# The first stage of a gated-MLP trunk kernel rebuilt: load order, the first modulation tile, and a written order on three engines

## The chip, the cores and the metric

One core of one Trainium2 chip runs the kernel. The metric is the device time of one execution in microseconds, median of the runs.

## The reference, cut to what matters

The input x has 2048 rows (tokens) of 1024 columns, in float32. With depth 1 the trunk is one layer with the chunked gMLP mixer:

```
mod = silu(c) @ ada_w + ada_b                  # 3072 values: shift, scale, gate
h   = rmsnorm(x, norm_g) * (1 + scale) + shift
u, v, z = split(h @ w_in, 3)                   # w_in: 1024 x 6144
u = gelu(u);  v = layernorm(gelu(v))
v = spatial mixing of v in chunks of 128 tokens, 8 heads
x = x + gate * ((u * v * silu(z)) @ w_out)
out = rmsnorm(x, final_g)
```

The stage that is changed is the beginning: from x, c and ada_w to h for the first 512 tokens, and the first products of h with w_in.

## The kernel before, in words

Every float32 product on TensorE is made from three matmuls (`mm3`, L175): each operand is split into a rounded part hi and a rest lo (`split`: hi by ACT, lo by DVE), and hi\*hi, hi\*lo and lo\*hi are summed in PSUM. The large products follow Strassen's scheme on quadrants of h and of the weights (A11, A12, A22 and the sums S1 to S4); the tokens are taken in two halves of 1024, and each of these in two halves of 512 (`HT`). The width of 1024 is cut into `KD` = 8 columns k of 128, of which k < 4 (`KH`) belong to A11 and the others to A12.

The first stage is the pool named "start". Its parts:

- **Rows.** c, norm_g and ada_b are loaded as rows and transposed by TensorE to columns; ACT makes c_act = silu(c) of them.
- **Modulation.** For each column k the 1024 x 128 blocks of ada_w for shift and scale are loaded by two transfers (`mod_load`, 1 MB in all, in three tiles used in turn). `mod_sum` multiplies the eight 128-row blocks by c_act and sums them: two products, by ACT (by DVE for k = 0), six multiply-adds and one add on DVE. Two small matmuls with a column of ones sum over the partitions into a PSUM tile pm; `mod_cols` turns pm into one scale and one shift column with three DVE instructions.
- **x.** Four chunks of 128 tokens (`load_half`) are normalised (`normalize_steps`: squares on ACT, a power on GpSimd, a scaling on DVE) and transposed by TensorE, column by column (`transpose_half`). `take_a1` copies the transposed column from PSUM; `modulate` (L249) applies scale and shift on ACT, and `put` splits the result h(k) into sh and sl.
- **Products.** For every k the weights of one 512-wide block of v and of two 128-wide blocks of u are loaded (`first_load`) and split (`first_split`). Four chunks and two units of u take three matmuls each, 18 matmuls a step, into six PSUM banks. After k = 3 the banks are evicted by ACT and started again for A12.

The order on DVE and ACT in this stage is the order of the program text (`tc.manual_schedule`, L747); TensorE's order and the order of the loads on SP's queue are made by the planner of the tile framework. In that text the sum for column k+2 stands in step k, the columns of k+1 are made in step k, and five x columns are transposed ahead of step 0. Loads are issued on SP's one queue: the rows, two ada tiles, four x chunks, then weights and ada tiles in turn; the second half of x (x2) is loaded in step 4.

Behind the stage come the second product group (`v1`, tiles named p_v), the normalisation of x2, and the rest of the program, which the edit doesn't touch.

Of the kernel before, what the change touches and what calls it, by code (L numbers as in the profile page):

```python
# [17 lines left out]
P = 128  # L18
# [4 lines left out]
def kernel(  # L23
# [192 lines left out]
    def mod_sum(j, aw):  # L216


        am = s_slot(A22, j % KH, "hl"[j // KH], F32, f"am_{j}", (P, 2, 2, P))
        for k in range(KD):  # L220
            a, ck = am[:, k % 2], c_act[:, k:k + 1]
            if k < 2 and j:
                nc.scalar.activation(a, aw[:, :, k, :], AF.Copy, scale=ck)
            elif k < 2:
                nc.vector.tensor_scalar(a, aw[:, :, k, :], ck, None, op0=ALU.mult)
            else:
                nc.vector.scalar_tensor_tensor(a, aw[:, :, k, :], ck, a, op0=ALU.mult, op1=ALU.add)
            if k in (3, 5, 6):
                yield None
        nc.vector.tensor_tensor(am[:, 0], am[:, 0], am[:, 1], op=ALU.add)  # L230
        pm = aux_bank(f"pm_{j}")
        for s in (1, 0):
            nc.tensor.matmul(
                pm[:, s:s + 1], lhsT=am[:, 0, s, :], rhs=ones[:, 0:1], start=True, stop=True
            )
        yield pm

    def mod_cols(cols, j, pm):
        nc.vector.tensor_tensor(
            mscale[:, j:j + 1], pm[:, 1:2], cols[:, R_SC + j:R_SC + j + 1], op=ALU.add  # L240
        )
        nc.vector.tensor_scalar(
            mscale[:, j:j + 1], mscale[:, j:j + 1], 1.0, cols[:, R_G + j:R_G + j + 1],
            op0=ALU.add, op1=ALU.mult,
        )
        nc.vector.tensor_tensor(
            mshift[:, j:j + 1], pm[:, 0:1], cols[:, R_SH + j:R_SH + j + 1], op=ALU.add
        )
# [461 lines left out]
    with tc.tile_pool(name="start", bufs=1) as st:  # L710
        nc.sync.dma_start(rows[R_C:R_C + KD, :], c.rearrange("o (k p) -> (o k) p", p=P))
        nc.sync.dma_start(
            rows[R_G:R_G + KD, :], norm_g.rearrange("o (k p) -> (o k) p", p=P)
        )
        nc.sync.dma_start(
# [3 lines left out]
        ps_r = aux_bank("ps_rows")  # L719
        nc.tensor.transpose(ps_r[:, :NR], rows[:NR, :], ident[:NR, :NR])  # L720
        nc.scalar.activation(c_act, ps_r[:, R_C:R_C + KD], AF.Silu)
        nc.vector.tensor_copy(cols, ps_r[:, :NR])
# [11 lines left out]
        v0, v1 = groups[0]  # L734

        def take_a1(k):
            ps = transpose_half(xh, 0, k, acc_bank if k < 5 else aux_bank)
            t = s_slot(S4, k % KH, "hl"[k // KH], F32, f"a1_{k}")
            if k == 0:
                modulate(t, ps, k)  # L740
            elif k in (1, 3):
                nc.vector.tensor_copy(t, ps)
            else:
                nc.scalar.activation(t, ps, AF.Copy)
            a1.append(t)

        with tc.manual_schedule(engines={mybir.EngineType.DVE, mybir.EngineType.Activation}):  # L747
            *_, pm[0] = mod_sum(0, aws[0])
# [571 lines left out]
```

## Time and profile before

| | before |
|---|---|
| time, median of 3 runs | 1341.31 us (1339.07 to 1345.71) |
| the profiled execution's own time | 1339.62 us |
| its span, first to last instruction | 1337.5 us |
| PE busy | 1309.9 us (98%) |
| DVE busy | 1073.9 us (80%) |
| ACT busy | 681.7 us (51%) |

The span is what the rows below are timed in: 0 is the first instruction of the profiled execution. PE is TensorE's matmuls, PEld its weight loads, DVE is VectorE, ACT is ScalarE, POOL is GpSimd and SPq the queue from which loads and stores are issued. A matmul's duration contains its pipeline; how fast matmuls follow is read from the distance of their starts. An instruction's line is often that of a helper: all splits are L166 and L167, all products L176 to L178.

### The profile page before, as it was taken

The page shows a single profiled execution, that of the slowest core. Times are in us where ns is not written, and L with a number is a line of the kernel's source. Part 1 is how long each engine was busy: PE and PEld are TensorE (multiplying, and loading weights), DVE is VectorE, ACT ScalarE, POOL GpSimd, SP SyncE. Part 2 cuts the span into 40 slices and gives each one's busy share as a digit, 9 for nine tenths or more (in the row PEclk, how much of TensorE's full clock was granted, in tenths as well). Part 3 has the DMA queues.
Part 4 walks back from the last instruction along what each step waited for, and adds up shares of the span by engine and source line. Part 5 has one row for each costly group of instructions (what it writes and reads, how often), then busy time and mean ns, then how long its engine had stood idle before and what let it go on. Part 6 is the DMA issues. An engine that isn't in the chain of part 4 may idle for free.

```text
span 1337.5 us, 17181 instructions
## 1 busy us (share of the span) xinstructions
PE 1309.9 (98%) x6066; PEld 1087.3 (81%) x6066; DVE 1073.9 (80%) x1784; ACT 681.7 (51%) x1169; POOL 25.0 (2%) x42
## 2 busy tenths in 40 slices
PE   5999999999999999999999999999999999999997
PEld 4878878888888888888888888888888888888876
DVE  6889978888888888978678889887789944757974
ACT  5775445766555537534345545544543424344553
POOL 0000001000000000000000000000000000000101
PEclk9999999999999999999999999999999999999999
DMA  9871657456765547442244345433339722335723
GB/s 320 274 263 56 227 193 239 149 171 203 232 231 186 177 154 238 168 135 104 102 142 133 116 163 176 158 111 118 122 124 311 257 95 95 99 120 213 252 105 126
DMA packets 156798, 229.23 MB, mean 171 GB/s; under 512 B 9188, under 2 KB 91172, under 8 KB 153384
## 3 DMA queue, kind: packets, MB, share of 16 engines
q1 hardware_dynamic: 156712, 228.14, 50.0%
q8 instruction: 47, 0.77, 0.2%
q14 instruction: 39, 0.32, 0.1%
HBM read 160.47 MB, written 67.64 MB: 171 GB/s over the span
## 4 chain that ended last, share of the span: by engine, by line
PE 76%; DVE 4%; DMA 2%; ACT 1%; issue 1%; POOL 0%; POOLq 0%; ACTq 0%
PE p_z L178 7%; PE p_z L177 7%; PE p_z L176 7%; PE po L178 7%; PE po L177 7%; PE po L176 7%; PE p_u L178 6%; PE p_u L177 6%; PE p_u L176 6%; PE pmix_u L550 4%; PE p_v L176 3%; PE p_v L178 3%; PE p_v L177 3%; DMA vn<-v_dram 1%; DMA sl<-h_dram 1%
## 5 line engine op out<-in xcount | busy, mean ns | idle before, releaser
L176 PE MATMUL p_v<-hi_p_v,sh 128*128 128x512 f32 x416 | 162.8, 392 | 0.1
L177 PE MATMUL p_v<-lo_p_v,sh 128*128 128x512 f32 x416 | 162.5, 391 | 0.0
L178 PE MATMUL po<-hi_o,gl 128*128 128x512 f32 x416 | 161.9, 389 | 0.5 <-DVE gl L167 0.5
L178 PE MATMUL p_v<-hi_p_v,sl 128*128 128x512 f32 x416 | 162.2, 391 | 0.0
L176 PE MATMUL po<-hi_o,gh 128*128 128x512 f32 x416 | 161.9, 389 | 0.0
L177 PE MATMUL po<-lo_o,gh 128*128 128x512 f32 x416 | 161.8, 389 | 0.0
L166 ACT ACTIVATE gh<-gr 128x1024 fp32r<-128x1024 f32 x52 | 55.0, 1059 | 132.5 <-PE po L177 123.2
L166 ACT ACTIVATE hi_p_v<-b_v 128x512 fp32r<-128x512 f32 x104 | 65.0, 630 | 106.7 <-PE p_v L178 89.8
L167 DVE TENSOR_TENSOR gl<-gr,gh 128x1024 fp32r<-128x1024 f32 x52 | 63.6, 1223 | 60.4 <-ACT gh L166 60.2
L167 DVE TENSOR_TENSOR lo_p_v<-b_v,hi_p_v 128x512 fp32r<-128x512 f32 x104 | 70.0, 688 | 37.2 <-ACT hi_p_v L166 36.8
L176 PEld LDWEIGHTS p_v<-hi_p_v,sh 128*128 128x128 f32 x416 | 78.1, 188 | 17.4 <-DVE c_v L479 1.0
L178 PEld LDWEIGHTS po<-hi_o,gl 128*128 128x128 f32 x416 | 78.1, 188 | 17.0 <-DVE gl L167 1.0
L176 PEld LDWEIGHTS po<-hi_o,gh 128*128 128x128 f32 x416 | 78.1, 188 | 16.6 <-ACT gh L166 0.3
L177 PEld LDWEIGHTS p_v<-lo_p_v,sh 128*128 128x128 f32 x416 | 78.1, 188 | 16.5 <-issue 0.2
L177 PEld LDWEIGHTS po<-lo_o,gh 128*128 128x128 f32 x416 | 78.1, 188 | 16.2
L178 PEld LDWEIGHTS p_v<-hi_p_v,sl 128*128 128x128 f32 x416 | 78.1, 188 | 16.0
L536 ACT ACTIVATE vn<-vn,lm,lr 128x256 f32<-128x256 f32 x128 | 67.7, 590 | 27.4 <-DMA vn<-v_dram 18.1
L176 PE MATMUL p_u<-sh,hi_p_u 128*128 128x512 f32 x196 | 76.2, 389 | 0.0
L177 PE MATMUL p_u<-sl,hi_p_u 128*128 128x512 f32 x196 | 76.2, 389 | 0.0
L178 PE MATMUL p_u<-sh,lo_p_u 128*128 128x512 f32 x196 | 76.2, 389 | 0.0
L176 PE MATMUL p_z<-sh,hi_p_z 128*128 128x512 f32 x192 | 75.0, 391 | 0.0
L178 PE MATMUL p_z<-sh,lo_p_z 128*128 128x512 f32 x192 | 75.0, 391 | 0.0
(220 smaller groups left out, 3081.3 us busy)
## 6 DMA issues: line engine op xcount, KB each, us to landing
gr<-g_dram SPq DMA_DIRECT2D x26, 1024.0 KB, 4.8
b_v<-in_gm_w_in_dram SPq DMA_DIRECT2D x18, 1024.0 KB, 5.5
vn<-v_dram SPq DMA_DIRECT2D x16, 1024.0 KB, 6.1
raw_u<-in_gm_w_in_dram SPq DMA_DIRECT2D x16, 1024.0 KB, 5.0
raw_z<-in_gm_w_in_dram SPq DMA_DIRECT2D x16, 1024.0 KB, 5.1
v_dram<-c_v SPq DMA_DIRECT2D x44, 256.0 KB, 2.1
g_dram<-c_u SPq DMA_DIRECT2D x37, 256.0 KB, 2.1
aw<-in_ada_w_dram SPq DMA_DIRECT2D x16, 512.0 KB, 5.4
```

The costliest lines, as they stand in the source:

```text
L166: nc.scalar.activation(hi, src, AF.Copy)
L167: nc.vector.tensor_tensor(lo, src, hi.bitcast(F32), op=ALU.subtract)
L176: nc.tensor.matmul(ps, lhsT=sh, rhs=mh, start=first, stop=False)
L177: nc.tensor.matmul(ps, lhsT=sh, rhs=ml, start=False, stop=False)
L178: nc.tensor.matmul(ps, lhsT=sl, rhs=mh, start=False, stop=last)
L536: nc.scalar.activation(vt[:, ch, :], vt[:, ch, :], AF.Identity, bias=lm[:, ch:ch + 1], scale=lr[:, ch:ch + 1],)
L550: nc.tensor.matmul(pm[:, i * P:(i + 1) * P], lhsT=vt[:, m * (NCH // 2) + i, f * P:(f + 1) * P], rhs=spT[:, u.j, :], start=True, stop=True,)
```

## The change

The x chunks are loaded first, the rows go to ACT's queue, the first ada tile is loaded in four parts (scale before shift) and summed by TensorE alone: eight blocks times a c_act column, accumulated in PSUM. Column 1 is summed by both engines: DVE takes blocks 0 to 4, TensorE 5 to 7 and the two partial sums. The columns' additions of 1 are made once, and the shift column is added by ACT. For columns 0 and 1, hi of h is written by ACT directly from the transposed x in PSUM, and DVE makes the float32 h beside it (`h_at_once`); for the others ACT makes h from PSUM and h is then split (`h_in_turn`). The sum for column k+1 is finished in step k, and TensorE transposes column k+1 in step k too. The order on DVE, ACT and TensorE is that of the text. x2 is loaded in step 6 instead of step 4.

```diff
     def mod_load(pool, j):
...
-        for s in range(2):
-            nc.sync.dma_start(aw[:, s], ada_v[:, :, s * D + j * P:s * D + (j + 1) * P])
+        parts = [slice(0, KH), slice(KH, KD)] if j == 0 else [slice(0, KD)]
+        for s in (1, 0):
+            for ks in parts:
+                nc.sync.dma_start(aw[:, s, ks], ada_v[:, ks, s * D + j * P:s * D + (j + 1) * P])
...
+    def mod_init(j, by_act):
+        am[j] = s_slot(A22, j % KH, "hl"[j // KH], F32, f"am_{j}", (P, 2, 2, P))
+        for k in range(2):
+            src, ck = aws[j][:, :, k, :], c_act[:, k:k + 1]
+            if by_act:
+                nc.scalar.activation(am[j][:, k], src, AF.Copy, scale=ck)
             else:
+                nc.vector.tensor_scalar(am[j][:, k], src, ck, None, op0=ALU.mult)
+
+    def mod_acc(j, ks):
+        for k in ks:
+            a = am[j][:, k % 2]
+            nc.vector.scalar_tensor_tensor(
+                a, aws[j][:, :, k, :], c_act[:, k:k + 1], a, op0=ALU.mult, op1=ALU.add
+            )
+
+    def mod_add(j):
+        nc.vector.tensor_tensor(am[j][:, 0], am[j][:, 0], am[j][:, 1], op=ALU.add)
+
+    def mod_total(j, direct, parts):
+        pm[j] = aux_bank(f"pm_{j}")
         for s in (1, 0):
+            terms = [(aws[j][:, s, k, :], c_act[:, k:k + 1]) for k in direct]
+            terms += [(am[j][:, i, s, :], ones[:, 0:1]) for i in range(parts)]
+            for n, (w, m) in enumerate(terms):
+                nc.tensor.matmul(
+                    pm[j][:, s:s + 1], lhsT=w, rhs=m, start=n == 0, stop=n == len(terms) - 1
+                )
+
+    def mod_cols(j):
+        nc.vector.tensor_scalar(
+            mscale[:, j:j + 1], pm[j][:, 1:2], cols[:, R_SC + j:R_SC + j + 1],
+            cols[:, R_G + j:R_G + j + 1], op0=ALU.add, op1=ALU.mult,
         )
+        nc.scalar.activation(
+            mshift[:, j:j + 1], pm[j][:, 0:1], AF.Identity, bias=cols[:, R_SH + j:R_SH + j + 1]
         )
...
     with tc.tile_pool(name="start", bufs=1) as st:
-        nc.sync.dma_start(rows[R_C:R_C + KD, :], c.rearrange("o (k p) -> (o k) p", p=P))
+        nc.scalar.dma_start(rows[R_C:R_C + KD, :], c.rearrange("o (k p) -> (o k) p", p=P))
...
+        xh = load_half(st, 0)
         aws, wf, pm = {}, {}, {}
-        for k in range(2):
+        for k in range(3):
             aws[k] = mod_load(st, k)
-        xh = load_half(st, 0)
-        for k in range(3):
-            if k == 2:
-                aws[k] = mod_load(st, k)
             wf[k] = first_load(k)
...
+        def h_at_once(k):
+            hi, lo, a = h_slots(k)
+            nc.vector.tensor_scalar(
+                a, psx[k], mscale[:, k:k + 1], mshift[:, k:k + 1], op0=ALU.mult, op1=ALU.add
+            )
+            yield
+            modulate(hi, psx[k], k)
+            nc.vector.tensor_tensor(lo, a, hi.bitcast(F32), op=ALU.subtract)
+
+        def h_in_turn(k):
+            hi, lo, a = h_slots(k)
+            modulate(a, psx[k], k)
+            split(hi, lo, a)
...
+        manual = {mybir.EngineType.DVE, mybir.EngineType.Activation, mybir.EngineType.PE}
+        with tc.manual_schedule(engines=manual):
...
             for ch, xt in enumerate(xh):
+                normalize_x(xt, f"0_{ch}")
+                if ch < 3:
+                    turn_x(0, [ch])
+            mod_total(0, range(KD), 0)
+            turn_x(0, [3])
+            mod_cols(0)
+            take_psx(1)
+            steps = h_at_once(0)
+            next(steps)
+            w_v = split_w(wf[0][0], "wfv_0", (P, FB))
+            for _ in steps:
+                pass
+            ws.append((w_v, split_w(wf[0][1], "wfu_0", (P, NF, P))))
             for k in range(KD):
...
                 if k == 4:
-                    x2 = load_half(st, 1)
                     v1.load(0, 0, "raw0")
-                    v1.load(1, 0, "raw1")
...
+                if k == 0:
+                    for n in range(3):
+                        for ch in range(4):
+                            chunk(k, ch, [n])
+                        if n == 1:
+                            turn_x(1, range(4))
+                    mod_init(1, False)
+                    mod_acc(1, range(2, 5))
+                    mod_total(1, range(5, KD), 2)
+                    ws.append(first_split(1, wf[1]))
+                    mod_cols(1)
+                    for j in range(NF):
+                        unit(k, j)
+                    for _ in h_at_once(1):
+                        pass
+                    mod_init(2, True)
+                    mod_acc(2, range(2, 4))
+                    continue
+                if k + 1 < KD:
+                    take_psx(k + 1)
+                    turn_x(k + 1, range(4))
+                    mod_acc(k + 1, range(4, KD))
+                    mod_add(k + 1)
+                    ws.append(first_split(k + 1, wf[k + 1]))
+                if k == KD - 2:
+                    x2 = load_half(st, 1)
+                    v1.load(1, 0, "raw1")
+                if 2 <= k < KD - 2:
+                    mod_init(k + 2, True)
+                for ch in range(3):
+                    chunk(k, ch)
+                if k == 1:
+                    chunk(k, 3)
+                if k + 1 < KD:
+                    mod_total(k + 1, (), 1)
+                    mod_cols(k + 1)
+                    if 2 <= k < KD - 2:
+                        mod_acc(k + 2, range(2, 4))
+                    h_in_turn(k + 1)
+                    if k == 1:
+                        mod_init(k + 2, True)
+                        mod_acc(k + 2, range(2, 4))
+                if k > 1:
+                    chunk(k, 3)
                 for j in range(NF):
+                    unit(k, j)
```

`turn_x` transposes chunks of one column, `chunk` and `unit` are the three matmuls of one chunk or one unit, `h_slots` takes the tiles of h(k).

## Rows read from the trace of the kernel before

**Rows 1.** The page's busy time: engine, us (share of the span), instructions.

```profile
PE 1309.9 (98%) x6066; PEld 1087.3 (81%) x6066; DVE 1073.9 (80%) x1784; ACT 681.7 (51%) x1169; POOL 25.0 (2%) x42
```

**Rows 2.** Busy time by stretches: stretch, length, engines, granted clock, DMA share, GB/s.

```profile
7.00:7.50 0.50, 0.00 (x0) 0.00 (x0) 0.21 (x1) 0.00 (x0) 0.00 (x0) 1.00 1.14 345
...
13.50:14.00 0.50, 0.00 (x0) 0.00 (x0) 0.30 (x1) 0.50 (x3) 0.46 (x1) 1.00 1.01 418
...
22.00:26.00 4.00, 3.56 (x9) 2.85 (x10) 3.62 (x11) 2.90 (x7) 0.00 (x0) 1.00 1.12 349
...
26.00:61.00 35.00, 35.00 (x173) 29.31 (x172) 31.09 (x82) 26.54 (x50) 0.00 (x0) 1.00 0.91 299
```

**Rows 3.** Timeline of all engines, 0 to 17 us: start, duration, engine, line, operation.

```profile
0.74 0.40 SPq L711 DMA_DIRECT2D rows<-in_c_dram  x1
...
1.89 3.75 SPq L213 DMA_DIRECT2D aw<-in_ada_w_dram  x4
...
7.29 0.61 DVE L225 TENSOR_SCALAR am<-aw,c_act 128x256 f32<-128x256 f32 x2 [3.33 <-DMA aw<-in_ada_w_dram]
...
10.79 0.93 PEld L233 LDWEIGHTS pm<-ones,am 128*128 128x128 f32 x4 [7.41 <-DVE am L230]
...
12.12 1.06 ACT L155 ACTIVATE sq<-x 128x1024 bf16<-128x1024 f32 x1 [8.39 <-DMA x<-in_x_dram]
...
15.30 1.33 PE L267 MATMUL psx<-ident,x 128*128 128x128 f32 x5 [3.50 <-DVE r_m L147]
...
16.96 1.32 PE L267 MATMUL psx<-ident,x 128*128 128x128 f32 x5 [0.33 <-DVE r_m L147]
```

**Rows 4.** Timeline of PE, 22 to 62 us: first product to the next stage.

```profile
22.44 0.80 PE L176 MATMUL p<-hi_wfv,sh 128*128 128x512 f32 x1 [0.68 <-ACT sh L166]
...
25.96 0.40 PE L178 MATMUL p<-hi_wfv,sl 128*128 128x512 f32 x1
...
28.24 0.50 PE L233 MATMUL pm<-ones,am 128*128 128x1 f32 x4
28.60 0.64 PE L267 MATMUL psx<-ident,x 128*128 128x128 f32 x4
28.99 0.48 PE L176 MATMUL p<-hi_wfv,sh 128*128 128x512 f32 x1
...
61.04 0.39 PE L176 MATMUL p_v<-hi_p_v,sh 128*128 128x512 f32 x1
```

**Rows 5.** Timeline of ACT, 20 to 46 us.

```profile
20.95 0.78 ACT L251 ACTIVATE a<-psx,mshift,mscale 128x512 f32<-128x512 f32 x1 [2.11 <-PE psx L267]
...
29.77 0.62 ACT L166 ACTIVATE hi_wfv<-wfv 128x512 fp32r<-128x512 f32 x1
...
30.59 0.90 ACT L223 ACTIVATE am<-aw,c_act 128x256 f32<-128x256 f32 x2
31.39 0.81 ACT L251 ACTIVATE a<-a,mshift,mscale 128x512 f32<-128x512 f32 x1
32.23 0.63 ACT L166 ACTIVATE sh<-a 128x512 fp32r<-128x512 f32 x1
...
42.83 2.04 ACT L483 ACTIVATE c_v<-p 128x512 f32<-128x512 f32 x4
...
45.70 0.66 ACT L166 ACTIVATE hi_wfv<-wfv 128x512 fp32r<-128x512 f32 x1
```

**Rows 6.** Timeline of DVE, 28 to 33 us.

```profile
28.23 0.68 DVE L167 TENSOR_TENSOR sl<-a,sh 128x512 fp32r<-128x512 f32 x1
28.83 0.15 DVE L239 TENSOR_TENSOR mscale<-pm,cols 128x1 f32<-128x1 f32 x1
...
29.21 1.67 DVE L227 SCALAR_TENSOR_TENSOR am<-aw,c_act,am 128x256 f32<-128x256 f32 x4
...
32.19 0.87 DVE L227 SCALAR_TENSOR_TENSOR am<-aw,c_act,am 128x256 f32<-128x256 f32 x2
```

**Rows 7.** Timeline of ACT: the squares of the second half of x.

```profile
63.92 1.04 ACT L155 ACTIVATE sq<-x 128x1024 bf16<-128x1024 f32 x1
```

More of the change, by code (lines that the diff above doesn't have):

```diff
@@ L734 @@
         v0, v1 = groups[0]
[L736 to L748, printed above, removed]
-            mod_cols(cols, 0, pm[0])
-            sums = mod_sum(1, aws[1])
-            for ch, xt in enumerate(xh):
-                norm = normalize_steps(xt, f"0_{ch}")
-                next(norm)
-                pm[1] = next(sums)
-                next(norm)
-            ws = [first_split(k, wf[k]) for k in range(2)]
-            for k in range(5):
-                take_a1(k)
-                if k == 0:
-                    put(0, A11, 0, a1[0])
+        ws, psx = [], {}
@@ new lines, in take_psx, with turn_x, h_slots @@
+        def take_psx(k):
+            psx[k] = (acc_bank if k == 0 else aux_bank)(f"psx_0_{k}")
+            return psx[k]
+        def turn_x(k, chs):
+            for ch in chs:
+                nc.tensor.transpose(
+                    psx[k][:, ch * P:(ch + 1) * P], xh[ch][:, k * P:(k + 1) * P], ident
+                )
+        def h_slots(k):
+            i = A11 if k < KH else A12
+            hi = s_slot(i, k % KH, "h", F32R, f"sh_0_{i}_{k % KH}")
+            lo = s_slot(i, k % KH, "l", F32R, f"sl_0_{i}_{k % KH}")
+            S[i][k % KH] = (hi, lo)
+            a1.append(s_slot(S4, k % KH, "hl"[k // KH], F32, f"a1_{k}"))
+            return hi, lo, a1[k]
@@ new lines, in h_at_once, with chunk @@
+        def h_at_once(k):
+            hi, lo, a = h_slots(k)
+            nc.vector.tensor_scalar(
+                a, psx[k], mscale[:, k:k + 1], mshift[:, k:k + 1], op0=ALU.mult, op1=ALU.add
+            )
+            yield
[5 more added lines that the diff above has]
+            split(hi, lo, a)
+        def chunk(k, ch, passes=range(3)):
+            sh, sl = S[A11 if k < KH else A12][k % KH]
+            cs = slice(ch * P, (ch + 1) * P)
+            hi, lo = ws[k][0]
+            for n in passes:
+                l, r = ((sh, hi), (sh, lo), (sl, hi))[n]
+                nc.tensor.matmul(
+                    first[ch], lhsT=l[:, cs], rhs=r, start=k % KH == 0 and n == 0,
+                    stop=k % KH == KH - 1 and n == 2,
+                )
@@ new lines, in unit @@
+        def unit(k, j):
+            sh, sl = S[A11 if k < KH else A12][k % KH]
+            hi, lo = ws[k][1]
+            mm3(first[4 + j], hi[:, j], lo[:, j], sh, sl, k % KH == 0, k % KH == KH - 1)
+        manual = {mybir.EngineType.DVE, mybir.EngineType.Activation, mybir.EngineType.PE}
+        with tc.manual_schedule(engines=manual):
+            ps_r = aux_bank("ps_rows")
+            nc.tensor.transpose(ps_r[:, :NR], rows[:NR, :], ident[:NR, :NR])
+            nc.scalar.activation(c_act, ps_r[:, R_C:R_C + KD], AF.Silu)
+            nc.vector.tensor_copy(cols, ps_r[:, :NR])
+            nc.vector.tensor_scalar(
+                cols[:, R_SC:R_SC + KD], cols[:, R_SC:R_SC + KD], 1.0, None, op0=ALU.add
+            )
+            take_psx(0)
+            for ch, xt in enumerate(xh):
+                normalize_x(xt, f"0_{ch}")
[11 more added lines that the diff above has]
+            ws.append((w_v, split_w(wf[0][1], "wfu_0", (P, NF, P))))
@@ L790 @@
                     first = [acc_bank(f"p{k // KH + 1}_{j}") for j in range(4 + NF)]
-                sh, sl = S[i][k % KH]
-                edges = k % KH == 0, k % KH == KH - 1
-                for ch in range(4):
-                    cs = slice(ch * P, (ch + 1) * P)
-                    mm3(first[ch], sh[:, cs], sl[:, cs], *ws[k][0], *edges)
+                if k == 0:
[16 more added lines that the diff above has]
+                    continue
```

54 lines of the change are left out of this document (3 added, 51 removed).

## The prediction

> **What bounds the kernel now.** I read the page first, then the busy time by stretches, then the order of the work on each engine up to 62 us. TensorE is busy 1309.9 of the 1337.5 us of the span [rows 1], so all that any change of order can give back is 27.6 us, and most of that lies at the head. The stretches show it: from 22 to 26 us PE is busy for 3.56 of 4.00, from 26 to 61 for 35.00 of 35.00 [rows 2]. The first matmul of the stage starts at 22.44 and the first one of the stage behind it at 61.04 [rows 4]; everything behind 61.04 is untouched by the edit, so the question is where 61.04 goes. It is the sum of two things: when the first matmul starts, and how closely the eight steps k = 0..7 follow.
>
> Both parts have their own limit. The start waits for data and for a serial chain: ada_w lands and DVE begins at 7.29, x only at 12.12, behind it in the one queue, PE transposes from 15.30 [rows 3]. The steps are limited by PE itself: 28.99 to 61.04 for k = 1..7 is 4.58 us a step [rows 4], where 18 matmuls at 0.228 (25.96 to 28.24, ten of them [rows 4]) make 4.10 and the rest is pm and transposes. DVE is close behind: 31.09 of 35 us [rows 2].
>
> **The start after the change.** The x loads take the first place in the queue, at 0.74 instead of behind the row loads and ada_w. Fixed cost of a load: the 1.05 MB of the first ada tile went out at 1.89, were used at 7.29, and take 3.04 us at 345 GB/s, which leaves 2.4 [rows 2, 3]. So the first x chunk (0.52 MB at 418 GB/s, 1.25 us) is there at 0.74 + 2.4 + 1.25 = 4.4. From the start of its squares to its first transpose it was 12.12 to 15.30, 3.2 us; the next chunk followed 1.65 behind [rows 3]. The written order puts chunks 0 to 2 ahead of mod_total(0): 4.4 + 3.2 + 2 x 1.65 + 0.3 for the transpose = 11.2. The first ada tile is there by 0.74 + 2.4 + 5.0 + 3.0 = 11.2, its scale half 1.5 earlier, so the load is no later than PE needs it. The three row loads move to ACT's queue; their issue (0.74 to 1.89, 1.2 us [rows 3]) and the table load end before x lands, so they cost nothing, and if x came early they would cost at most those 1.2.
>
> What DVE did in 3.4 us is now PE's: 8 blocks, 2 sums, two passes each (the trace shows 4 records for the two products of one pm) = 32 passes. At the high level of the clock a pass is 0.09 (28.24 to 28.60 for four), at the low level 0.23 by the four at 10.79 to 11.72 [rows 3, 4]. Which level holds? Matmuls start 0.44 apart from 22.44 to 25.96 (eight) and 0.228 apart behind that [rows 4]: those are the 1.2 and 2.4 GHz levels, although the granted-clock column reads 1.00 in both stretches [rows 2]. Bounds of the 32 passes: 2.9 and 7.4. I take 0.18, twice the high-level pass, hence 5.8, and no slow matmuls behind: pm_0 is done at P = 17.0. Behind P come the two column operations (0.3, an estimate from the 0.15 at 28.83 [rows 6] and a handover), hi of the weights (0.62, as at 29.77 [rows 5]) and hi of h straight from PSUM (0.78, as at 20.95 [rows 5]): first matmul at P + 1.7 = 18.7, 3.7 earlier than before. That is the gain.
>
> **The steps after the change.** Call S(k) the moment at which hi of h(k) is ready. Step 0: 12 matmuls 2.74, the transposes of chunk column 1 at 0.39 (28.60 to 28.99 [rows 4]), then pm_1 with 20 passes, 1.8: P + 6.6; DVE's part (lo of h and of w, two products, three sums: 4.5 from P) lies beside it. Then columns 0.3, hi 0.78: S(1) = P + 7.7.
>
> From there the written order makes a ring over DVE and ACT, because pm(k+1) is now summed, used and turned into h(k+1) within one step; before, pm ran a step ahead. Ring: lo of h(k) on DVE 0.60 (28.23 to 28.83), four sums, add, lo of both weights 2.98 (29.21 to 32.19) [rows 6], scale column and handover 0.2, modulate 0.84 and hi 0.63 on ACT (31.39, 32.23 [rows 5]), handover 0.05: 5.3 us. PE's work of the step is 18 x 0.228 + pm 0.36 + transposes 0.39 = 4.85, so PE now waits about 0.45 a step (at mod_total, with chunk 3, both units and the next transposes queued behind it, which nothing but h(k+1) waits for), and it pays seven times 0.39 for transposes behind the first matmul where it paid three.
> In steps 1 and 2 the order has no sums ahead: ACT's two products (0.80, 30.59 to 31.39 [rows 5]) and two more sums (0.83) come into the ring, less lo of h that lies beside the products: 0.05 + 0.80 + 0.83 + 2.98 + 0.2 + 1.47 = 6.3 each. In step 4 six banks are evicted on ACT ahead of the weight splits: 2.87 (42.83 to 45.70), then hi of both weights 0.82, products 0.80, shift column 0.2, modulate and hi 1.47 [rows 5]: 6.2. Before, the same eviction cost PE nothing, since pm was a step ahead.
> So S(7) = P + 7.7 + 2 x 6.3 + 3 x 5.3 + 6.2 = P + 42.4. Step 7: 0.65 until lo is ready, then 16 x 0.228 = 3.65. The stage ends at P + 46.7 = 63.7, against 61.04: 2.7 us later. The start gives 3.7, the steps lose 6.4.
>
> Taken from DVE: one of three column operations per step (0.15 to 0.21) and the two copies; the ring already leaves them out. The ada reloads wait for tiles that are read a little later, but each has 5 us or more until its use; cost nothing, at worst one transfer of 3.0 once. The second half of x moves from k = 4 to k = 6, behind the last transposes: issue at about S(6) = 54 (SP holds the stores behind it for so long; they free tiles that nothing asks for before the next stage), last chunk 54 + 2.4 + 5.0 = 61.4; in the old order its squares start 2.9 behind the stage's end (63.92 [rows 7]), so at 66.6: hidden by 5 us.
>
> The profiled execution took 1339.62 us, 1.7 under the median of 1341.31. 1339.6 + 2.7 = 1342.3 on its scale; on the median's scale **1344.0 us**.
>
> **The rivals.**
> *The ring doesn't bind (faster).* If DVE and ACT kept up, PE would set the pace: P + 1.7 + 6.3 + 6 x 4.85 + 4.1 = P + 41.2. With the clock up halfway through the 32 passes (16 x 0.18 + 16 x 0.09 = 4.3, P = 15.5) that is 56.7, 4.3 earlier: 1337.0. With all passes at 0.09 it is 55.3: 1335.6, the most that the change can give. For it: PE was never seen waiting from 26 to 61. Against it: then no ring was closed within a step, and its members are measured.
> *The clock rises early, the ring stays.* P = 15.5, stage end 62.2: 1342.5. For it: the passes follow one another without a gap. Against it: the PE busy share before 22.44 was high too (transposes), and the matmuls behind it were slow.
> The Trainium skill (TensorE: Matmul & The Clock Gate, Part 1: The HAM clock gate) has the gate opened by sustained PE activity, which speaks for this rival; its Part 4: PE-mode transpose says that transposes don't count as busy in the same way, and the trace agrees with that, since the matmuls at 22.44 came at 0.44. No run here shows how one-column passes count.
> *Slower: the clock stays low until the dense matmuls have run for a while.* Place: pm_0 and step 0. Passes at 0.23 put P at 18.6, and eight matmuls at 0.44 instead of 0.228 add 1.7: stage end 67.0, 6.0 later, 1347.3. It decides from the point where S(1) lies beyond 26.9. For it: the 0.93 for four passes at 10.79 and the slow eight at 22.44 [rows 3, 4].
> *The second half of x is late.* It must now cross the queue in 7 us; if the 1 MB weight loads that wait for ada tiles stand ahead of it in the queue (two, 3.0 each by the rate above), it lands at 67.4, about 1 behind its use, and PE, which meets the transposes in order, waits for the chain of 3.2: 1345 to 1348.
>
> **How the numbers follow.** Forecast 0.50, its own range 1341 to 1347.5; ring not binding 0.12; early clock 0.15; low clock 0.15; late x 0.08. About 0.5%, 6.7 us, is what a measurement of this kernel can tell from no change: under 1334.6 is faster, over 1348.0 slower. Faster needs the very limit of the first rival (0.03 of its 0.12, and 0.01 for what I have not seen); slower gets 0.04 of the forecast, 0.06 of the low clock and 0.03 of the late x. That is faster 0.04, slower 0.13, no change 0.83. The range goes from the first rival's 1337.0 to 1350.0, the low clock with 0.4 us more in each of the seven rings.
>
> **What would show it.** First matmul of the stage near 18.7; the first x squares near 4.4; 32 passes between 11 and 17; DVE or ACT named as PE's releaser once a step, with 5.3 between the starts of steps 3, 5 and 6 and over 6 in 1, 2 and 4; the stage behind starting near 63.7. A first matmul before 16, or steps of 4.85, would make the prediction wrong towards faster; PE waiting for x transposes behind 64, towards slower.

## The result and the profile after

The changed kernel takes 1353.72 us (median of 4 runs, 1353.43 to 1354.29), the kernel before 1341.40 (4 runs, 1339.07 to 1345.71): ratio 1.0098, 95% interval 1.0083 to 1.0113. It is 12.3 us slower, where 2.7 were forecast, and beyond the 1350.0 at which the range ended. The profiled execution took 1354.29 us with a span of 1352.5, 15.0 more than before.

Busy time, as in [rows 1]:

```profile
PE 1321.5 (98%) x6110; PEld 1094.8 (81%) x6110; DVE 1069.1 (79%) x1758; ACT 679.0 (50%) x1168; POOL 24.7 (2%) x42
```

PE is busy 11.6 us longer with only 44 instructions more. The sum doesn't tell why; the distances of the starts do. Timeline of PE (start, duration, line, tile; in brackets the wait ahead of it), answering to [rows 3, 4]:

```profile
6.06 0.28 PE L793 MATMUL ps_rows<-ident,rows 32*128 32x32 f32 x1 [6.06 <-DMA rows<-in_ada_b_dram]
9.26 0.47 PE L747 MATMUL psx<-ident,x 128*128 128x128 f32 x1 [2.92 <-DVE r_m L147]
...
12.56 6.83 PE L249 MATMUL pm<-c_act,aw 128*128 128x1 f32 x32
19.24 0.45 PE L747 MATMUL psx<-ident,x 128*128 128x128 f32 x1
21.71 2.08 PE L780 MATMUL p<-hi_wfv,sh 128*128 128x512 f32 x4 [2.01 <-ACT sh L263]
...
27.55 0.72 PE L249 MATMUL pm<-c_act,aw 128*128 128x1 f32 x6
...
32.36 0.78 PE L780 MATMUL p<-hi_wfv,sh 128*128 128x512 f32 x1
...
74.42 0.39 PE L176 MATMUL p_v<-hi_p_v,sh 128*128 128x512 f32 x1
```

The first product comes at 21.71, only 0.73 earlier than before; step 1 starts at 32.36, 3.37 later; the stage behind starts at 74.42 instead of 61.04. So 13.4 of the 15.0 us arise in this stage. Of the rest, 1.2 is a longer wait for DVE in the second half of x (2.1 us against 0.9); the remaining 0.4 is not traced.

The stretches (engine columns PE, PEld, DVE, ACT, POOL, then granted clock, DMA share, GB/s), as [rows 2]:

```profile
12.00:19.00 7.00, 6.71 (x32) 6.71 (x33) 1.05 (x3) 0.00 (x0) 0.55 (x1) 1.00 1.14 355
...
21.50:27.50 6.00, 5.79 (x16) 4.68 (x17) 3.67 (x9) 1.28 (x4) 0.00 (x0) 1.00 0.67 212
27.50:29.70 2.20, 2.20 (x22) 2.15 (x21) 0.00 (x0) 0.00 (x0) 0.00 (x0) 1.00 0.00 0
...
30.60:33.90 3.30, 3.30 (x12) 2.60 (x11) 2.45 (x5) 2.40 (x5) 0.00 (x0) 0.50 1.00 296
...
36.00:74.00 38.00, 34.11 (x158) 24.90 (x157) 28.75 (x66) 25.19 (x51) 0.00 (x0) 1.00 0.76 247
```

Three things are to be seen. While TensorE sums column 0 (12 to 19 us) DVE and ACT do next to nothing, and while it sums column 1 (27.5 to 29.7) everything else stands still. Behind the passes of column 1 the granted clock is 0.50, the 1.2 GHz level, and there the products start 0.43 apart (30.80 to 31.23 to 31.66). The twelve products behind column 0 start 0.43 apart too, though the column reads 1.00 for them (21.5 to 27.5): this trace has no record of the clock ahead of 27.18, the column shows 1.00 where there is none, and at 27.2 the distance falls to 0.24. So these twelve ran at the low level as well. And from 36 to 74 PE is busy for 34.11 of 38.00 us, where it was 35.00 of 35.00.

ACT, as [rows 5, 7]:

```profile
6.38 0.18 ACT L794 ACTIVATE c_act<-ps_rows 128x8 f32<-128x8 f32 x1 [3.04 <-PE ps_rows L793]
6.45 1.05 ACT L155 ACTIVATE sq<-x 128x1024 bf16<-128x1024 f32 x1
...
30.18 0.26 ACT L258 ACTIVATE mshift<-pm,cols 128x1 f32<-128x1 f32 x1 [7.40 <-DVE mscale L254]
31.33 0.78 ACT L263 ACTIVATE sh<-psx,mshift,mscale 128x512 fp32r<-128x512 f32 x1 [0.88 <-DVE a L762]
...
37.93 0.63 ACT L166 ACTIVATE sh<-a 128x512 fp32r<-128x512 f32 x1
...
67.13 0.63 ACT L166 ACTIVATE hi_p_v<-b_v 128x512 fp32r<-128x512 f32 x1 [3.50 <-PE p L780]
67.67 0.24 ACT L258 ACTIVATE mshift<-pm,cols 128x1 f32<-128x1 f32 x1
...
69.14 0.62 ACT L166 ACTIVATE sh<-a 128x512 fp32r<-128x512 f32 x1
...
77.88 1.04 ACT L155 ACTIVATE sq<-x 128x1024 bf16<-128x1024 f32 x1
```

and DVE, as [rows 6]:

```profile
29.87 0.28 DVE L254 TENSOR_SCALAR mscale<-pm,cols 128x1 f32<-128x1 f32 x1 [4.51 <-PE pm L249]
30.48 0.81 DVE L762 TENSOR_SCALAR a<-psx,mscale,mshift 128x512 f32<-128x512 f32 x1 [0.33 <-ACT mshift L258]
```

The pair of views shows the chain behind pm_1, the PSUM tile with the sums of column 1 (done at 29.70): scale column 29.87, shift column 30.18, float32 h on DVE 30.48, and only when that has ended hi on ACT, 31.33 to 32.11. "At once" it is not: the two readers of one PSUM tile come one after the other. The ends of sh give S(k), the moments at which hi of h(k) is ready: S(1) = 32.11, S(2) = 38.56 (the row at 37.93), S(3) to S(6) 45.02, 50.68, 57.14, 62.80, and S(7) = 69.76 (the row at 69.14). In the last interval ACT stands at the weight split of the next stage (67.13, 3.50 of waiting for PE) with the shift column of 7 queued behind it; a second such split stands at 68.62 between h(7) and its hi.

### The profile page after: what moved, and what is told of

It reads as the page before. It is cut to its first block, busy times and chain, and to the rows that moved or that the text cites. A ratio compares the mean times of both kernels' runs of the same rounds, so it can differ in the third digit from the quotient of the medians.

```text
span 1352.5 us, 17256 instructions
## 1 busy us (share of the span) xinstructions
PE 1321.5 (98%) x6110; PEld 1094.8 (81%) x6110; DVE 1069.1 (79%) x1758; ACT 679.0 (50%) x1168; POOL 24.7 (2%) x42
## 4 chain that ended last, share of the span: by engine, by line
PE 88%; DVE 5%; DMA 3%; ACT 2%; issue 1%; POOL 1%; SPq 0%; ACTq 0%; POOLq 0%; DVEq 0%
PE p_z L178 7%; PE p_z L176 7%; PE p_z L177 7%; PE po L178 7%; PE po L176 7%; PE po L177 7%; PE p_u L178 7%; PE p_u L177 7%; PE p_u L176 7%; PE p_v L177 6%; PE p_v L176 6%; PE p_v L178 6%; PE pmix_u L562 4%; PE pm L249 1%; DMA wfu<-in_gm_w_in_dram 1%
## 5 line engine op out<-in xcount | busy, mean ns | idle before, releaser
L548 ACT ACTIVATE vn<-vn,lm,lr 128x256 f32<-128x256 f32 x128 | 67.6, 589 | 28.8 <-DMA vn<-v_dram 19.6
```

What stands on the lines that cost most here:

```text
L548: nc.scalar.activation(vt[:, ch, :], vt[:, ch, :], AF.Identity, bias=lm[:, ch:ch + 1], scale=lr[:, ch:ch + 1],)
```

## The experiments

Stage end is the start of the first matmul of p_v (61.04 before, 74.42 after), from each kernel's profiled execution; the ratio is to the kernel before. The times of one kernel scatter by up to 6 us (1357.30 to 1363.50 in e1_ahead), so a kernel with one run is read by its stage end alone. What lies behind the stage end took 1274 to 1281 us in these executions (span less stage end): a stage end shows what the stage costs, and differences of 2 or 3 us between the times needn't come from it. Thus e11_order, whose stage ends 1.5 us before that of e7_mend, has a median 2.0 above it.

| kernel | median us | ratio, 95% interval | stage end |
|---|---|---|---|
| e1_ahead | 1361.14 | 1.0145 (1.0123 to 1.0168) | 77.8 |
| e2_dense | 1354.81 | 1.0097 (1.0079 to 1.0115) | 75.6 |
| e3_hi_first | 1356.39, one run | | 73.5 |
| e4_rows_first | 1354.66, one run | | 73.4 |
| e5_ring | 1347.76 | 1.0051 (1.0034 to 1.0068) | 66.9 |
| e6_dve0 | 1348.72 | 1.0058 (1.0045 to 1.0071) | 71.0 |
| e7_mend | 1344.88 | 1.0034 (1.0026 to 1.0043) | 66.7 |
| e8_before_x | 1342.96 | 1.0016 (1.0007 to 1.0024) | 64.6 |
| e9_clock | 1348.39, one run | | 70.5 |
| e10_warm | 1340.80 | 0.9996 (0.9986 to 1.0006) | 61.8 |
| e11_order | 1346.84 | 1.0045 (1.0028 to 1.0062) | 65.2 |

My theory: the ring of DVE and ACT within a step takes the most, and the one-column passes with the low clock most of the rest. The rival: the low clock is nearly all of it.

**e1_ahead: the sum one step ahead, first try.** The sum of k+2 is made in step k, but its add stands behind the lo of h(k+1) on DVE.

```diff
+                    mod_cols(k + 1)
+                    if k + 2 < KD:
+                        mod_init(k + 2, True)
                     ws.append(first_split(k + 1, wf[k + 1]))
+                    if k + 2 < KD:
+                        mod_acc(k + 2, range(2, 5))
...
                     h_in_turn(k + 1)
...
+                if k + 2 < KD:
+                    mod_acc(k + 2, range(5, KD))
+                    mod_add(k + 2)
+                unit(k, 0)
+                if k + 2 < KD:
+                    mod_total(k + 2, (), 1)
+                unit(k, 1)
```

> The sum for column k+2 is finished in step k again, a step ahead of its use, with TensorE's order else as in the changed kernel. Theory 'ring' (summing, using and turning a column into h inside one step closes a loop over DVE and ACT): steps 1 to 6, which took 6.45, 6.46, 5.66, 6.46, 5.66 and 6.96 us from hi of h(k) to hi of h(k+1), fall to PE's own 4.9 to 5.1 each, the stage ends at 66 to 68 instead of 74.4, the run is 6 to 8 us shorter than the changed kernel. Rival 'late data' (the ada tiles are what each step waits for): the steps stay near 5.7 and the stage ends within 1 us of 74.4.

It became slower still, against the expectation. PE's waits from 20 to 78 us (what it waited for: us in total, times, longest):

```profile
PE pm L249 <- DVE am L240: 8.6, 5, 3.0
```

pm(k+2) now needs an add that stands behind h(k+1), and h(k+2) needs pm(k+2): the ring is still closed within a step and has become longer: the scale columns of two steps start at 46.12 and 53.27, 7.15 apart. This says nothing against the ring; it was the wrong cut.

By chance this run shows something else. TensorE's text is that of the changed kernel up to pm_1, but in this execution the clock rose earlier:

```profile
25.29 1.17 PE L780 MATMUL p<-hi_wfv,sl 128*128 128x512 f32 x4
26.30 0.72 PE L249 MATMUL pm<-c_act,aw 128*128 128x1 f32 x6
```

The last four of the twelve products come at 0.23 and pm_1 starts at 26.30 instead of 27.55. S(1) is 30.87 instead of 32.11: what the low clock costs ahead of pm_1 goes in full into S(1).

**e5_ring: the same, cut rightly.** The columns of k+1 are the first thing in step k, from a sum finished in step k-1.

```diff
                     turn_x(k + 1, range(4))
-                    mod_acc(k + 1, range(4, KD))
-                    mod_add(k + 1)
+                    if k == 1:
+                        mod_total(2, (), 1)
+                    mod_cols(k + 1)
+                    if k + 2 < KD:
+                        mod_acc(k + 2, range(2, KD))
+                        mod_add(k + 2)
+                    h_in_turn(k + 1)
                     ws.append(first_split(k + 1, wf[k + 1]))
...
+                unit(k, 0)
+                if k + 2 < KD:
+                    mod_total(k + 2, (), 1)
+                unit(k, 1)
```

> The first try at a sum one step ahead still closed a loop: its add stood behind lo of h(k+1), and ACT's products and weight splits stood between the columns and h. Here the column of k+1 is made at the start of step k from a sum finished in step k-1, h(k+1) follows at once, and the sum for k+2 stands ahead of lo of h(k+1). Theory 'ring': steps 1 to 6 take 4.9 to 5.3 us each instead of 6.45, 6.46, 5.66, 6.46, 5.66, 6.96; the stage ends at 66 to 69 instead of 74.4; the run is 5 to 8 us shorter than the changed kernel. Rival 'late data or banks': steps stay at 5.6 or more, no gain over 2 us.

Stage end 66.9. Up to S(1), 32.07 here, everything is as in the changed kernel, the low clock too, so 7.5 us of the 13.4 are the ring. This refutes the rival, for which the clock is nearly all of it. From step 2 on PE sets the pace; two of its pm rows, one step apart:

```profile
42.09 0.50 PE L249 MATMUL pm<-ones,am 128*128 128x1 f32 x4
...
47.12 0.50 PE L249 MATMUL pm<-ones,am 128*128 128x1 f32 x4
```

The step is 5.03 us, and from 20 to 67 PE waits only once, 2.0 us ahead of the first product. Before, a step was 4.58 in the mean [rows 4], but the single steps differ there (first products of steps 2 to 5):

```profile
34.03 0.48 PE L176 MATMUL p<-hi_wfv,sh 128*128 128x512 f32 x1
...
39.05 0.48 PE L176 MATMUL p<-hi_wfv,sh 128*128 128x512 f32 x1
...
43.73 0.39 PE L176 MATMUL p<-hi_wfv,sh 128*128 128x512 f32 x1
...
48.28 0.40 PE L176 MATMUL p<-hi_wfv,sh 128*128 128x512 f32 x1
```

A step with the transposes of a column takes 5.02, one without them 4.68 or 4.55. So PE's step became no slower; in the changed order every step but the last has transposes, where before only the first ones had.

**e6_dve0: no one-column sums.** Columns 0 and 1 are summed by DVE; pm_0 and pm_1 take four passes each, as before.

```diff
-            mod_total(0, range(KD), 0)
+            mod_acc(0, range(2, KD))
+            mod_add(0)
+            mod_total(0, (), 1)
...
-                    mod_acc(1, range(2, 5))
-                    mod_total(1, range(5, KD), 2)
+                    mod_acc(1, range(2, KD))
+                    mod_add(1)
+                    mod_total(1, (), 1)
```

> Columns 0 and 1 are summed by DVE as before; TensorE's 32 and 20 passes are gone but for four each. Everything else is as in the changed kernel. Theory 'passes' (32 one-column passes at the low clock cost more than DVE's free time, and those of column 1 drop the clock again): pm_0 is done 1.5 to 2 us earlier than 19.4, pm_1 takes 0.4 to 0.8 instead of 2.2, no matmul of step 1 is slow, hi of h(1) at 28 to 30 instead of 32.1, the stage ends 2.5 to 4 earlier than 74.4. Rival 'DVE is the late engine': hi of h(1) no earlier than 31.5.

```profile
16.80 1.02 PE L249 MATMUL pm<-ones,am 128*128 128x1 f32 x4 [2.36 <-DVE am L240]
20.14 2.07 PE L780 MATMUL p<-hi_wfv,sh 128*128 128x512 f32 x4 [2.32 <-ACT sh L263]
...
25.98 0.50 PE L249 MATMUL pm<-ones,am 128*128 128x1 f32 x4
```

The first product is 1.6 earlier than with the passes, pm_1 takes 0.36 instead of 2.15, no product of step 1 is slow, and the stage ends 3.4 earlier: the 1.6 and the 1.8 of pm_1. Letting TensorE sum these two columns was a loss.

**e2_dense: keep the passes, feed the clock.** Dense bf16 matmuls, whose result is not used, ahead of the transposes, between the passes and in the gap ahead of the first product.

```diff
                 nc.tensor.matmul(
                     pm[j][:, s:s + 1], lhsT=w, rhs=m, start=n == 0, stop=n == len(terms) - 1
                 )
+                if len(terms) > 1 and n % 2:
+                    dummy(1)
...
             turn_x(0, [3])
+            dummy(7)
```

> Dense dummy matmuls (512 columns, bf16, into a bank that nobody reads) stand ahead of the x transposes, between the one-column passes and in the gap behind them; nothing else is changed. Theory 'low clock' (one-column passes leave the clock at its low level): the 32 passes take 3 to 5 us with the dummies instead of 6.7, the twelve matmuls of step 0 follow at 0.23 instead of 0.43, none of step 1 is slow; hi of h(1) comes 4 to 6 us earlier than 32.1 and the stage ends 4 to 6 us earlier than 74.4. Rival 'cost of the passes themselves' (weight loads, not the clock): the passes keep their 0.21 and the dummies only add, the stage ends 0 to 3 us later.

The profile here is of the slowest of its four runs (1358.59). Its stretches:

```profile
12.00:24.00 12.00, 11.58 (x48) 9.28 (x50) 3.25 (x8) 2.21 (x5) 0.55 (x1) 0.50 0.88 275
...
26.00:31.00 5.00, 4.92 (x36) 4.52 (x36) 1.14 (x4) 0.00 (x0) 0.00 (x0) 1.00 0.14 43
```

One dense matmul for four passes did not raise the clock: 0.50 from 12 to 24, and the additions cost 2.3 us until the first product (24.04). The seven behind them did better: twelve products and four transposes take 4.04 instead of 5.84. A like mixture from 28.1 to 30.7, the passes of pm_1 with four dense matmuls among them (three show in the records), began with the clock up, and it stayed up: 1.00 there and no slow product in step 1. That the dense matmuls kept it is not shown, for in e1_ahead it stayed up without them. In sum the gain doesn't pay for the additions, and the stage ends 1.2 later.

**e9_clock: the clock alone, on e6_dve0.** Twelve dense matmuls around pm_0; the lines are against e6_dve0.

```diff
             mod_add(0)
+            dummy(8)
             mod_total(0, (), 1)
+            dummy(4)
```

> The kernel after with columns 0 and 1 summed by DVE (as in e6_dve0, first p_v 71.0) and twelve dense bf16 matmuls, which the result doesn't need, around the four passes of pm_0, and nothing else. Theory 'the low clock was only in the way where PE was the limit': the twelve products of step 0 start 0.23 apart instead of 0.43 and end about 2.4 us earlier, but DVE's sum of column 1, which doesn't get faster, then ends last (as in e7_mend), so hi of h(1) is ready at 28 to 28.7 against 28.75 and the stage ends at 70.0 to 71.0. Rival 'the low clock was itself the cost': hi of h(1) by 26.5, stage end 68.6 or less.

```profile
20.54 1.20 PE L788 MATMUL p<-hi_wfv,sh 128*128 128x512 f32 x4 [0.78 <-ACT sh L263]
...
24.96 0.61 PE L249 MATMUL pm<-ones,am 128*128 128x1 f32 x4 [0.95 <-DVE am L240]
```

The twelve products come at 0.23, but behind them PE waits for DVE's sum, which didn't get faster: hi of h(1) at 28.00 against 28.75, stage end 70.5. Where DVE makes the sums, the high clock is worth 0.5 to 0.7 us here, less what the dense matmuls cost themselves (the first product comes 0.4 later than in e6_dve0); in the changed kernel, where the twelve products and then the passes end last, the low clock costs its whole difference, as e1_ahead shows.

**e3_hi_first: ACT's hi ahead of DVE's float32 h.** For column 0 the split of the first weights is also written ahead of both.

```diff
+            modulate(hi, psx[k], k)
             nc.vector.tensor_scalar(
                 a, psx[k], mscale[:, k:k + 1], mshift[:, k:k + 1], op0=ALU.mult, op1=ALU.add
             )
             yield
-            modulate(hi, psx[k], k)
```

> In h_at_once ACT's hi comes ahead of DVE's float32 h, only the order of the two readers of the PSUM tile is turned. Theory 'one reader of a bank at a time' (the two reads were made to wait for each other): DVE now waits for ACT's hi, first matmul about 0.4 earlier, hi of h(1) 0.8 earlier after the column, but the ring through DVE's lo and sums keeps its time, so the stage ends 0.3 to 0.6 earlier. Rival 'both read at once': hi and float32 h overlap in the trace, and the order makes no difference to either.

The first product comes 0.46 earlier (21.25) and the stage ends 0.9 earlier, but not all of that is the order: the clock rose earlier in this execution, and the twelve products and four transposes took 5.19 instead of 5.84, which is 0.65. For column 1 ACT and DVE, in that order:

```profile
29.38 0.78 ACT L263 ACTIVATE sh<-psx,mshift,mscale 128x512 fp32r<-128x512 f32 x1
```

```profile
30.19 0.81 DVE L763 TENSOR_SCALAR a<-psx,mscale,mshift 128x512 f32<-128x512 f32 x1 [1.14 <-ACT sh L263]
```

Now DVE waits for ACT. Whoever reads first, the other starts when it has ended. The rest of h(1), which the ring needs, ends no sooner for it: DVE starts it 2.44 behind pm_1 in both kernels (31.03 here, 32.14 there).

**e4_rows_first: the row loads back on SP's queue, ahead of x.**

```diff
-        nc.scalar.dma_start(rows[R_C:R_C + KD, :], c.rearrange("o (k p) -> (o k) p", p=P))
+        nc.sync.dma_start(rows[R_C:R_C + KD, :], c.rearrange("o (k p) -> (o k) p", p=P))
...
```

> The three row loads go back to SP's queue ahead of x. Theory 'rows behind x' (issued on ACT's queue beside x they landed at 6.0 instead of 3.2, and silu of c stands ahead of the first squares on ACT): silu by 3.8, first squares at 5.4 to 5.8 when x lands, the 32 passes begin 0.6 to 1 us earlier than 12.56 and the stage ends as much earlier. Rival 'x itself': the first squares stay at 6.4 or come later by the 1.2 us of issue.

```profile
3.10 0.28 PE L793 MATMUL ps_rows<-ident,rows 32*128 32x32 f32 x1 [3.10 <-DMA rows<-in_ada_b_dram]
...
11.79 6.83 PE L249 MATMUL pm<-c_act,aw 128*128 128x1 f32 x32
```

The rows are there 3 us sooner (3.10 against 6.06), the passes start 0.77 earlier, the stage ends 1.1 earlier; the twelve products with their transposes took 5.56 here, so 0.3 of it is again the clock.

**e7_mend: all of these together.** The ring of e5_ring, the sums of e6_dve0, dense matmuls, rows first, hi first.

> All suspected costs taken out at once, with x still loaded ahead of ada_w: rows first on SP, columns 0 and 1 summed by DVE, ACT's hi ahead of DVE's float32 h, the sum one step ahead as in the run above, and dense dummy matmuls in PE's idle time ahead of the first product. If the causes are independent and complete: first product at 18 to 20, its twelve matmuls 0.23 apart, hi of h(1) near 25, steps of 5.0 to 5.3, stage end 58 to 61, run 1338 to 1342, within 0.2% of the kernel before. If something else costs the time: stage end over 64, run over 1344.

A miss: 66.7 instead of 58 to 61. The first product is at 18.61 and the twelve come at 0.23, but DVE's order is wrong for the earlier start:

```profile
24.68 2.46 DVE L235 SCALAR_TENSOR_TENSOR am<-aw,c_act,am 128x256 f32<-128x256 f32 x6
...
27.51 0.27 DVE L254 TENSOR_SCALAR mscale<-pm,cols 128x1 f32<-128x1 f32 x1
```

The sum of column 2 stands ahead of the columns of 1 (pm_1 was done at 24.35). PE idles for 1.80 us ahead of pm_1 and for 2.18 and 1.09 behind it, and the products of step 1 come at 0.43.

**e11_order: e7_mend with DVE's order mended.** Column 1 sooner, h(1) ahead of the next sum, and column 2 summed by TensorE between the chunks of step 1. The lines are against e7_mend.

```diff
             mod_add(0)
+            mod_init(1, True)
+            mod_acc(1, range(2, 4))
...
+                        for n in range(4):
+                            chunk(1, n)
+                            s = 1 if n < 2 else 0
+                            for kk in range(4 * (n % 2), 4 * (n % 2) + 4):
+                                nc.tensor.matmul(
+                                    pm[2][:, s:s + 1], lhsT=aws[2][:, s, kk, :],
+                                    rhs=c_act[:, kk:kk + 1], start=kk == 0, stop=kk == KD - 1,
+                                )
+                        mod_cols(2)
```

> e7_mend (first p_v 66.7) with three moves: two products (by ACT) and two multiply-adds of column 1 go into DVE's idle time behind the add of column 0; columns and h of 1 stand ahead of the sum of column 2; column 2 is summed by TensorE alone, 32 one-column passes between the chunks of step 1, so that DVE has one sum less. Theory 'e7_mend lost to the written order on DVE': the sum of column 1 ends near 22.4 (23.8 in e7_mend), hi of h(1) is ready at 24.5 (28.9), no product of step 1 comes at 0.43, the sum of column 3 is ready in step 1, then steps of 4.8 to 5.0 and a stage end of 60 to 62: 1339 to 1342 us, ratio to before 0.999 to 1.001. Rival 'DVE has too much work in the stage, whatever the order': hi of h(1) as above, but steps of 5.0 to 5.5 with PE waiting for DVE in each, stage end 63 to 66, 1342 to 1346 us. If the passes between products take 0.21 and let the clock fall, step 1 ends some 4 us later, stage end 64 to 65.

65.2: neither theory. All that PE waits for from 19.6 to 66 us:

```profile
PE p L788 <- DMA aw<-in_ada_w_dram: 0.6, 1, 0.6
PE pm L249 <- DVE am L240: 0.5, 1, 0.5
PE p L788 <- DVE lo_wfv L167: 0.3, 1, 0.3
PE p L788 <- ACT sh L263: 0.3, 1, 0.3
PE p L788 <- ACT hi_wfv L166: 0.2, 1, 0.2
```

That is 1.9 us, no wait for DVE in the later steps, the clock is up throughout, and still the stage ends 4.2 later than before. So now it is PE's own work. One of its later steps, from first product to first product:

```profile
46.87 0.48 PE L788 MATMUL p<-hi_wfv,sh 128*128 128x512 f32 x1
...
51.88 0.48 PE L788 MATMUL p<-hi_wfv,sh 128*128 128x512 f32 x1
```

Steps 1 to 7 take 39.26 us (25.94 to 65.20) where they took 32.05, 7.2 more: the 32 passes are 3.2 (four times 0.80), waits 1.1, and steps 3, 4 and 5, which now have transposes (5.05, 5.01, 5.04 for 4.68, 4.55, 4.55), 1.3; the other 1.6, nearly all in steps 1 and 2, are not put down to rows. The first product is 2.8 earlier (19.68 for 22.44) and step 0 is 0.3 shorter, which pays 3.1 of the 7.2.

**e8_before_x and e10_warm: the idea of the change in the kernel before.** e8_before_x loads x between the first two ada tiles; e10_warm leaves the loads and puts 14 float32 matmuls, whose result is not used, ahead of the first product.

```diff
-        for k in range(2):
-            aws[k] = mod_load(st, k)
+        aws[0] = mod_load(st, 0)
         xh = load_half(st, 0)
+        aws[1] = mod_load(st, 1)
```

```diff
             *_, pm[0] = mod_sum(0, aws[0])
+            dummy(8, am0[0][:, 0, 0])
...
+            for xt in xh[:3]:
+                dummy(2, xt[:, 0:P])
```

> The kernel before with the load order alone: x stands between the first and the second ada tile, and the second tile is summed behind the normalisation instead of between its parts; everything else as before. Theory 'the start is worth what x comes earlier': squares near 9.1 instead of 12.1, first product at 19.3 to 20.3 instead of 22.44, stage end 58 to 60 instead of 61.0, run 1 to 3 us under the kernel before. Rival 'DVE takes it back' (the second sum, moved behind, delays step 1): first product earlier, stage end within 0.5 of 61.0, run the same.

> The kernel before with eight float32 128x128 matmuls (their result is not used) in TensorE's idle time behind pm_0, and six more among the x transposes ahead of the first product; the planner also puts the transposes of the first two chunks together. Nothing else is changed. Before, TensorE is the bound from 22.44 on and its first eight products start 0.44 apart. Theory 'where TensorE is the bound the low clock costs its full difference': most of the eight come at 0.23, the first product starts at 22.3 to 22.9, the stage ends at 59.4 to 60.6 (61.04 before), 1338.8 to 1340 us, ratio 0.9985 to 0.9995. Rival 'DVE takes it back, as in e8_before_x': products at 0.23 but a wait for DVE's pm_1 or h(1) behind them, stage end 60.7 to 61.3, ratio 1.000. Rival 'transposes among them keep the clock low': products at 0.44 again, stage end 61.0 to 61.8.

e8_before_x, PE:

```profile
21.04 0.79 PE L176 MATMUL p<-hi_wfv,sh 128*128 128x512 f32 x1 [1.35 <-ACT sh L166]
...
25.76 0.50 PE L233 MATMUL pm<-ones,am 128*128 128x1 f32 x4
...
30.07 0.61 PE L233 MATMUL pm<-ones,am 128*128 128x1 f32 x4 [2.15 <-DVE am L230]
```

e10_warm, PE:

```profile
23.75 0.50 PE L176 MATMUL p<-hi_wfv,sh 128*128 128x512 f32 x1 [0.65 <-ACT sh L166]
...
28.89 0.60 PE L235 MATMUL pm<-ones,am 128*128 128x1 f32 x4 [0.77 <-DVE am L232]
29.74 0.47 PE L176 MATMUL p<-hi_wfv,sh 128*128 128x512 f32 x1
```

In e8_before_x the first product is 1.40 earlier, but the stage ends at 64.6, 3.6 later than before: neither expectation had that. The row at 25.76 is pm_1, so the wait of 2.15 is for the sum of column 2. DVE makes the sum of column 1 from 21.75 on, where the edit put it, behind the normalisation; before, it began at 13.70, between the parts of it. The tile for column 1 lands later too, at 16.20 instead of 10.25, but that is still 4.7 us ahead of its first use at 20.89. So the sum of column 2, which stands behind it, is ready only at 30.02. Behind the idle time the clock falls: eight products of step 1 come 0.43 apart from 31.96 to 34.95, and the granted clock is 0.67 in the mean from 30.5 to 34.5.

In e10_warm all the first products come at 0.23, but they begin 1.3 later, because the last transposes of x start at 21.94 instead of 20.45, behind added matmuls. DVE's work behind h(0) starts 1.3 later with it, and PE waits 0.77 for the sum of column 2; step 1 starts 0.75 later than before. Both times DVE ends last and takes the gain back, and no version beat the kernel before.

## Why the prediction was wrong

The direction of the steps was right (start earlier, steps longer, a net loss), the size was not: the stage end is 10.7 us beyond the 63.7 forecast. By the prediction's own steps:

| step | forecast | measured | excess |
|---|---|---|---|
| passes of mod_total(0) start | 11.2 | 12.56 | 1.36 |
| the 32 passes | 5.8 | 6.68 | 0.88 |
| P to first product | 1.7 | 2.47 | 0.77 |
| first product to S(1) | 6.0 | 10.40 | 4.40 |
| S(1) to S(7) | 34.7 | 37.65 | 2.95 |
| S(7) to stage end | 4.3 | 4.66 | 0.36 |

**The step that failed is the one to S(1)** ("no slow matmuls behind", "columns 0.3, hi 0.78"). Two terms of it were mis-sized. First the clock: twelve products and four transposes took 5.84 instead of 3.13, and pm_1 2.15 instead of 1.8. This was the rival "the clock stays low"; it was the true case, its terms (1.6 for the passes and 1.7 for slow products) measured 0.9 and 2.7. I had given it 0.15; S(1) at 32.11 is well beyond the 26.9 from which it was to decide, a bound whose working the prediction doesn't show. What spoke for it stood in [rows 3, 4]: four one-column passes at 0.93, and products at 0.44 behind a TensorE that had been busy with transposes. Its size is in part luck of the execution: the same twelve products and four transposes took 4.67 in e1_ahead, 5.19 in e3_hi_first, 5.56 in e4_rows_first, 5.80 in e5_ring and 5.84 here, by when the clock rose.

Second the chain behind pm: priced 1.1, measured 2.41. It is four instructions in a row on two engines, scale 0.28, shift 0.26, float32 h 0.81, hi 0.78, with handovers; I had counted two of them, taking the columns as parallel and the two forms of h too. The same chain behind pm_0 (19.24 to 21.66) takes 2.42, and that is the excess of 0.77 in the row "P to first product". The Trainium skill (PSUM — Partial Sum Buffer, section "PSUM bank collisions raise a hardware error") says that two engines may not touch one bank in the same partitions at once, readers included, and that software has to keep them apart; the traces agree, since DVE's read waited for ACT's in e3_hi_first and ACT's for DVE's in the changed kernel, and no run lets both read at once. The rule was to be had ahead of the prediction and speaks against this very part. The same serial columns (scale at its start to hi at its end, 36.52 to 38.56 in step 1, is 2.04, priced 1.67) are 0.37 of each later step.

**The start.** The squares were forecast at 4.4 and came at 6.45, and that is not x: its second, third and fourth chunk were used from 5.71, 6.96 and 8.18 on, 1.25 apart, so the first was there at about 4.5, an estimate from these. The squares waited for silu, which stands ahead of them on ACT and needs the rows; the rows landed at 6.06, beside 2 MB of x on the other queue. "They cost nothing", and "at most those 1.2" if x came early, failed: the squares come about 2 us late. (From there to the first transpose at 9.26 it took 2.8 instead of 3.2, and on to the passes 3.3 instead of 3.6, so 1.36 is left in the table.) With the rows ahead of x on SP's queue (e4_rows_first) x itself comes later, the squares start at 5.67, and 0.8 is won. The Trainium skill (DMA: Bandwidth & Descriptors, section "Issuing engines are not separate DMA queues") says that transfers from all queues interleave on the same engines; the 6.06 against 3.10 fits that, but no run separates the other queue from the place behind x.

**The ring** was foreseen: 6.45, 6.46, 5.66, 6.46, 5.66 against 6.3, 6.3, 5.3, 6.2, 5.3. What was not is step 6: 6.96 for 5.3, because ACT's split of the next stage's weights waits for a slot with the shift column of 7 behind it (about 0.95), and a second such split stands between h(7) and its hi (0.37). e5_ring prices the ring at 7.5 us, the largest single cause. My 4.85 for PE's own step was 5.03; the kernel before has the same 5.02 in its steps with transposes, which its mean of 4.58 hid.

**The late x** was not the main cause: its squares start at 77.88, 3.5 behind the stage end (2.9 before), and what lies behind the stage end is 1.6 of the 15.0 us, 1.2 of it the wait named above. "The ring doesn't bind" is refuted by e5_ring.

The single cuts of e5_ring, e6_dve0, e4_rows_first and e3_hi_first give 7.5, 3.4, 1.1 and 0.9; added up, 12.9 of the 13.4, of which about 0.9 is the earlier rise of the clock in the last two. They are not independent, as e7_mend shows: with all of them the stage end is 66.7, since the bound goes to DVE, and with DVE's order mended to PE. What stays open is 1.6 us of steps 1 and 2 in e11_order, and why the clock rises at different moments in executions of the same text.

## What to carry to other kernels

An edit that starts a stage earlier is worth only what the engine that comes next can follow: before pricing the start, look what each engine did in the time that is to be cut away (here DVE made its sums while x landed, and with x first it made them later). When the product of a chain is pulled into the step that uses it, write down every instruction of the closed ring, with two readers of one PSUM tile one after the other, and compare it with the step; cut it by using in step k only what step k-1 finished. Small work moved to TensorE is priced at the low clock unless a row of its own shows the high one, and two executions of one text needn't have the clock up at the same moment: a gain of under 1 us in a stage is read against that.

## What was not expected of the hardware

- One-column passes keep the PE row busy (6.71 of 7.00 us) and yet 32 of them ran at the low level to their end: 0.21 a pass, and products at 0.43 behind them. At the high level a pass takes 0.11 (27.55 to 29.70 for twenty).
- Behind those twenty the granted clock was 0.50 (30.6 to 33.9), and e3_hi_first, e4_rows_first and e5_ring show the same. In e1_ahead it was not so: behind the same twenty passes, 26.30 to 28.45, products come at 0.23. That such passes bring the clock down is therefore not shown. In e11_order, with three products between every eight passes, it stayed high too.
- In executions with the same text on TensorE up to pm_1 the clock rises at different moments: at 24.60 in e1_ahead, at 27.11 in e5_ring and at 27.18 in the changed kernel.
- The granted-clock column reads 1.00 from 12 to 19 although the passes go at the low level, because the trace has no record of the clock there; the distances of the starts tell more than the column.
